# A three-block network on one core: bias tables written from all partitions, key sets joined by pairs of heads, and a scan's products ordered by kind

## The chip, the cores and the metric

The kernel runs on one core of a Trainium2 chip, as one program that a scheduler has laid out beforehand: each engine (TensorE for matmuls, VectorE, ScalarE, GpSimd, and SyncE, which issues DMAs) works off its own list in order and waits on semaphores for the others. The metric is the time of one execution on the device in microseconds. In rows PE is TensorE, PEld its weight loads, DVE VectorE, ACT ScalarE, POOL GpSimd, SP SyncE; a q behind a name is the queue of that engine's sequencer.

## What is computed

A residual block of dilated window attention and a state-space scan, then two blocks with two streams (512 latent tokens, 256 context tokens), the first with an rwkv scan, the second with an mLSTM. All is fp32. Three parts matter here. Attention has 24 heads in three groups of eight; a group has its own window, dilation and table of relative bias. The three groups' outputs of a head are joined by a softmax over their log denominators:

```python
logits = einsum('znqhd,znkhd->znhqk', qb, kw) * HEAD_DIM ** -0.5 + bias
m = max(logits); p = exp(logits - m); den = sum(p)
o, lse = (p @ v) / den, m + log(den)
...
alpha = softmax(stack(lses), axis=2)
attn = sum(alpha[..., None] * stack(outs), axis=2)      # (b, s, 8 * 64)
```

The bias of query i and key j depends on i - j alone (`rel_bias_g[bucket]`, -inf outside the window). The rwkv scan has eight heads of 64 and runs in both directions over the context (256 tokens) and then the latent stream (512):

```python
def step(s, inp):
    r_t, w_t, k_t, v_t, kk_t, b_t = inp
    sa = einsum('bhvk,bhk->bhv', s, kk_t)
    s = s * w_t[:, :, None, :] - sa[..., None] * b_t[:, :, None, :] + v_t[..., None] * k_t[:, :, None, :]
    return s, einsum('bhvk,bhk->bhv', s, r_t)
```

## The kernel before

Big products are split into high and low parts and taken as three matmuls (`mm3`, L301 to L303; `tok`, L384 to L386). `wload` brings a weight block of 128 x 1024 through three rotating buffers: SyncE loads `wraw` (0.52 MB), ScalarE casts `whi` (L292), VectorE subtracts `wlo` (L293). PSUM has eight banks: four in `psA`, two in `psB` and two in `psO`.

The stages, in us of the profiled span: norm to 22; the projection w_v of the values, 12 loads with 24 matmuls of 512 columns each, 22 to 112; the first pair's queries and keys (`qk`) to 160; the units of attention to 354; the join and the product w_ab to 409; the state-space part, its output and feed-forward to 1430; the rwkv scan 1430 to 2220; the rest to 3434. The scan's twelve steps (four of context, eight latent) are interleaved with feed-forward and projection work that a share in `mix0_scan` hands out; the rest of the order is the scheduler's.

**The tables.** `rel_bias` makes one line per head as a matmul of 33 rows (L446: `p` in 8 partitions, 384 or 256 columns), writes it 128 times to DRAM (`scr`, L449) and reads it back with a row length of one less, so that each partition's line is shifted by one (L452, L454: `B0`, `B12`). All of it is issued by GpSimd, beside the projection's loads.

**Attention.** A pair of heads (`hp`) has four units, two for each of two key sets: group 0's local windows, and groups 1 and 2 together. A unit's scores go through VectorE (bias and maximum, L483), ScalarE (exponential with sums), eight transposes on TensorE (L499), copies (L504) and the product with the values (L514). Maxima and sums of all eight heads collect in `st` (128 x 4 x 8 x 4), unnormalised outputs in `Os`. `merge` takes the units in turn with the next pair's `qk`, for the last pair with five of eight `gates`. Then `attn_join` transposes `st` (L585), writes it to DRAM and reads it with heads on partitions (L589, L591), makes weights 8 x 2 x 512 (L599 to L607), writes them (L609), broadcasts them to 64 partitions per head (L614) and joins the two sets (L617 to L619), split into `ah`, `al`. In the caller w_ab is a product of `ah`, `al` with four loads, two feature blocks each, four k-blocks per feature block, one k-block per pair.

**The scan.** A step has `scores` (products of keys and queries, and transposes by matmul with halves of the identity: `vs`, L1516, 16 of 64 columns, and `Ns`, L1527, 32), `inverse` (L1552, L1562, ten rounds of 16 small products) and `serial` (F, U, N and the output O). In rows a record of a 64-wide fp32 product stands twice, so 16 products are 32 records. O takes, for each of eight (direction, pair) blocks, two products with `Sc` (128 rows, L1618) and two with the state `S` (64 rows, L1620), each with its own start and stop:

```python
for d, b in DB:
    for e, h in enumerate(H):
        mm(O[h, d, b], Sc[:, d, e, b, 1], vu[:, d, e, b], start=True, stop=False, ...)
    for e, h in enumerate(H):
        mm(O[h, d, b], AR[d][h, b, 1], S[h, d, b], start=False, stop=True, ...)
```

## Time and profile before

| | us |
|---|---|
| median of three runs (3434.73 to 3446.99) | 3446.86 |
| the profiled execution | 3435.72 |
| its span | 3433.8 |
| TensorE busy | 3209.5 (93%) |
| VectorE, ScalarE, GpSimd busy | 2010.4, 1383.1, 226.9 |

The span leaves 1.9 us of the profiled execution outside. A record of TensorE begins when the product begins; records overlap, so the cost of one in a row of many is the distance from start to start. [...]

### The profile page before, as it was taken

To read this page: it belongs to the slowest core of one execution; us is meant where nothing else is said; L and a number is where in the kernel's file an instruction comes from. 1 tells how busy PE (TensorE), PEld (TensorE's weight loads), DVE (VectorE), ACT (ScalarE), POOL (GpSimd) and SP (SyncE) were. 2 spreads that over 40 slices of the span, in tenths; PEclk is the share of its full clock that TensorE was granted. 3 is DMA by queue.
4 is the path that set the end of the run, shared out by engine and by line. 5 is a ranking of instruction groups with operands and counts; after the bars stand their busy time and mean duration, and the time that the engine had idled before them with its cause. 6 is when DMAs were issued, how large, how long until landed. Compare 5 with 4: busy or idle time off the path is not lost.

```text
span 3433.8 us, 53206 instructions
## 1 busy us (share of the span) xinstructions
PE 3209.5 (93%) x21803; PEld 2567.3 (75%) x21803; DVE 2010.4 (59%) x3226; ACT 1383.1 (40%) x2294; POOL 226.9 (7%) x260
## 2 busy tenths in 40 slices
PE   6999799999889999889899999989999989899998
PEld 5877577777677788766577888767788767778887
DVE  2333567775645543556655656667565754766656
ACT  2233244342344442443344444446532444543323
POOL 0000000000100000022121121000000200000001
PEclk9999999999999999999899999999999989999999
DMA  7411343445444432434555544542322325232323
GB/s 135 128 62 62 109 140 128 135 148 177 148 138 136 128 111 98 139 119 119 151 164 164 169 160 137 177 168 89 108 95 92 133 95 172 89 105 92 98 92 111
DMA packets 216843, 430.96 MB, mean 126 GB/s; under 512 B 75426, under 2 KB 114546, under 8 KB 216344
## 3 DMA queue, kind: packets, MB, share of 16 engines
q1 hardware_dynamic: 193736, 370.09, 34.1%
q10 hardware_dynamic: 20464, 51.58, 4.0%
q0 software_dynamic: 2400, 5.90, 1.7%
q8 instruction: 171, 2.80, 0.3%
q14 instruction: 72, 0.59, 0.1%
HBM read 380.70 MB, written 46.79 MB: 124 GB/s over the span
## 4 chain that ended last, share of the span: by engine, by line
PE 77%; DVE 9%; DMA 7%; ACT 4%; issue 2%; POOL 0%; SPq 0%; ACTq 0%; POOLq 0%; DVEq 0%
PE psa L301 11%; PE psa L303 11%; PE psa L302 11%; PE psa L385 5%; PE psa L384 5%; PE psa L386 5%; PE pso L301 3%; PE pso L303 3%; PE pso L302 3%; DVE wlo L293 2%; DMA wraw<-in_w_v_dram 1%; PE psa L1552 1%; ACT whi L292 1%; PE psa L1562 1%; PE pso L1017 1%
## 5 line engine op out<-in xcount | busy, mean ns | idle before, releaser
L293 DVE TENSOR_TENSOR wlo<-wraw,whi 128x1024 fp32r<-128x1024 f32 x480 | 597.5, 1246 | 524.2 <-ACT whi L292 518.7
L292 ACT CAST whi<-wraw 128x1024 fp32r<-128x1024 f32 x482 | 503.7, 1046 | 773.0 <-PE psa L386 224.6
L301 PE MATMUL psa<-xh,wlo 128*128 128x512 f32 (+1 forms) x1760 | 693.3, 396 | 18.0 <-DVE wlo L293 10.7
L303 PE MATMUL psa<-xh,whi 128*128 128x512 f32 (+1 forms) x1760 | 684.7, 390 | 0.0
L302 PE MATMUL psa<-xl,whi 128*128 128x512 f32 (+1 forms) x1760 | 683.7, 389 | 0.0
L301 PEld LDWEIGHTS psa<-xh,wlo 128*128 128x128 f32 x1760 | 335.6, 192 | 97.6 <-DVE wlo L293 14.9
L303 PEld LDWEIGHTS psa<-xh,whi 128*128 128x128 f32 x1760 | 336.0, 191 | 72.7 <-issue 4.2
L302 PEld LDWEIGHTS psa<-xl,whi 128*128 128x128 f32 x1760 | 336.3, 191 | 71.6 <-issue 3.8
L1138 DVE SCALAR_TENSOR_TENSOR fc<-psa,f_cv,fc 128x441 f32<-128x441 f32 (+2 forms) x352 | 243.4, 692 | 41.4 <-ACT fc L1127 34.5
L301 PE MATMUL pso<-xh,wlo 128*128 128x256 f32 (+1 forms) x720 | 232.0, 322 | 0.6 <-ACT u L1445 0.5
L302 PE MATMUL pso<-xl,whi 128*128 128x256 f32 (+1 forms) x720 | 222.0, 308 | 1.0 <-DVE xl L347 1.0
L303 PE MATMUL pso<-xh,whi 128*128 128x256 f32 (+1 forms) x720 | 221.8, 308 | 0.0
L385 PE MATMUL psa<-wlo,ah 128*128 128x512 f32 x528 | 210.9, 399 | 2.8 <-DVE wlo L293 2.5
L384 PE MATMUL psa<-whi,al 128*128 128x512 f32 x528 | 209.0, 399 | 3.4 <-ACT whi L292 3.4
L386 PE MATMUL psa<-whi,ah 128*128 128x512 f32 x528 | 209.7, 398 | 0.0
L301 PEld LDWEIGHTS pso<-xh,wlo 128*128 128x128 f32 x720 | 137.0, 190 | 12.9 <-issue 1.7
L302 PEld LDWEIGHTS pso<-xl,whi 128*128 128x128 f32 x720 | 136.9, 190 | 9.6 <-DVE xl L347 1.6
L303 PEld LDWEIGHTS pso<-xh,whi 128*128 128x128 f32 x720 | 136.5, 190 | 8.2 <-issue 0.8
L384 PE MATMUL psa<-whi,xl 128*128 128x512 f32 x288 | 117.6, 410 | 19.3 <-ACT whi L292 16.0
L385 PEld LDWEIGHTS psa<-wlo,ah 128*128 128x128 f32 x528 | 99.0, 188 | 30.1 <-DVE wlo L293 6.3
L384 PEld LDWEIGHTS psa<-whi,al 128*128 128x128 f32 x528 | 98.8, 187 | 29.6 <-ACT whi L292 4.7
L385 PE MATMUL psa<-wlo,xh 128*128 128x512 f32 x288 | 117.2, 407 | 1.1 <-DVE wlo L293 1.1
(554 smaller groups left out, 5168.5 us busy)
## 6 DMA issues: line engine op xcount, KB each, us to landing
wraw<-in_f_up_dram SPq DMA_DIRECT2D x132, 512.0 KB, 3.8
wraw<-in_ada_w_dram SPq DMA_DIRECT2D x96, 512.0 KB, 3.6
wraw<-in_f_dn_dram SPq DMA_DIRECT2D x66, 512.0 KB, 3.5
wraw<-in_w_fi_dram SPq DMA_DIRECT2D x44, 512.0 KB, 3.5
wraw<-in_ab_f_dram SPq DMA_DIRECT2D x38, 512.0 KB, 3.8
wraw<-in_w_qk_dram SPq DMA_DIRECT2D x24, 512.0 KB, 3.7
wraw<-in_w_xbc_dram SPq DMA_DIRECT2D x24, 512.0 KB, 4.7
wraw<-in_c_f_dram SPq DMA_DIRECT2D x24, 512.0 KB, 4.3
```

The lines of the kernel that those rows point to most:

```text
L292: nc.scalar.copy(hi, raw)
L293: (eng or nc.vector).tensor_tensor(lo, raw, hi.bitcast(F32), op=ALU.subtract)
L301: mm(ps, wl, xh, start=start, stop=False)
L302: mm(ps, wh, xl, start=False, stop=False)
L303: mm(ps, wh, xh, start=False, stop=stop)
L384: mm(ps, sl, wh[:, c], start=first and k == 0, stop=False)
L385: mm(ps, sh, wl[:, c], start=False, stop=False)
L386: mm(ps, sh, wh[:, c], start=False, stop=last and k == kbn - 1)
L1017: nc.tensor.matmul(ps[o:o + 32], self.cs[:, 4 * h + j, 22 - 2 * i:54 - 2 * i], raw[:, j * 256:(j + 1) * 256], start=h == 0, stop=h == 1, t ...
L1138: V_.scalar_tensor_tensor(o, pv[:, r0 + dr:r1 + dr, c0 + dc:c1 + dc], cw(i), o, op0=ALU.mult, op1=ALU.add)
L1552: mm(ps[h, d, b], Al[h, d, b], Tm[h, d, b], start=True, stop=True, tile_position=(64 * e, 64 * e))
L1562: mm(ps[h, d, b], lt[h, d, b], rt[h, d, b], start=True, stop=True, tile_position=(64 * e, 64 * e))
```

## The change

Three parts. In `rel_bias` each head's line is replicated over 16 partitions before the matmul (`rep`, one copy of 33 x 24 x 16 more), so that the table stands in all 128 partitions, each of which writes 8 of a head's 128 copies. `attn_join` is called per pair: its statistics are 32 x 128, its tables 8 x 128 (head and chunk of 128 tokens on partitions), its DMAs are issued by ScalarE (one and four for `dstat`) and GpSimd; a pair's join is merged with the next pair's units, the last with the last four gates (four where five stood beside the last units). w_ab makes two rounds of two loads and four banks: three k-blocks for all four, then the last pair's k-block. In the scan O takes all `Sc` products and then all `S` products with one start and stop per bank, and `vs` and `Ns` are made with whole transposes of 128 x 128: 4 and 8 in place of 16 and 32 half ones; the copies of `vs` become four smaller ones, two of them on VectorE.

```diff
@@ rel_bias
-        tab, es = flat()[:NBUCKET + 1, :896], flat()[:8]
+        tab, es = flat()[:NBUCKET + 1, :896], flat()
+        rep = pool.tile([NBUCKET + 1, 24, 16], F32, name="pT", bufs=3)
+        nc.vector.tensor_copy(rep, lhs.unsqueeze(2).to_broadcast([NBUCKET + 1, 24, 16]))
...
-            ps = self.btile()[:8, :L]
-            nc.tensor.matmul(ps, lhs[:, g * 8:(g + 1) * 8], tab[:, off:off + L], start=True, stop=True)
+            ps = self.btile()[:, :L]
+            nc.tensor.matmul(ps, rep[:, g * 8:(g + 1) * 8].rearrange("k h r -> k (h r)"), tab[:, off:off + L], start=True, stop=True)
...
-            scr = self.dram.tile([8, P * L + 512], F32, name="scr%d" % g)
-            dst = scr[:, :P * L].rearrange("h (p l) -> h p l", l=L)
-            nc.gpsimd.dma_start(dst, e.unsqueeze(1).to_broadcast([8, P, L]))
+            scr = self.dram.tile([8, P * L], F32, name="scr%d" % g)
+            dst = scr.rearrange("h (r q l) -> (h r) q l", q=8, l=L)
+            nc.gpsimd.dma_start(dst, e.unsqueeze(1).to_broadcast([P, 8, L]))
@@ attention
             for hp in range(4):
-                merge(units(hp, *qk_[hp]), qk(hp + 1, *qk_[hp + 1]) if hp < 3 else islice(other, 5))
-          with self.tc.tile_pool(name="ac", bufs=2) as pool:
-              merge(self.attn_join(pool, st, Os, ah, al), other)
+                Os = op.tile([P, 2, SEQ], F32, name="Os", bufs=2)
+                merge(units(hp, *qk_[hp], Os), qk(hp + 1, *qk_[hp + 1]) if hp < 3 else islice(other, 4), join)
+                join = self.attn_join(op, hp, st[:, hp], Os, ah, al)
+          merge(join, other)
@@ attn_join, the part after the change
+        ps = self.btile()[:32, :P]
+        nc.tensor.transpose(ps, st.rearrange("p a e c -> p (a e c)"), self.ident)
+        sT = pool.tile([32, P], F32, name="sT")
+        S_.copy(sT, ps)
+        dst = self.dram.tile([4, 2, 4, P], F32, name="dstat%d" % hp)
+        S_.dma_start(dst[0:2].rearrange("a e c p -> (a e c) p"), sT[0:16])
+        for x in range(4):
+            S_.dma_start(dst[2 + x // 2, x % 2].rearrange("c (r i) -> r c i", r=4),
+                         sT[16 + 4 * x:20 + 4 * x].rearrange("r (c i) -> r c i", c=4))
+        yield
+        R = pool.tile([8, 4, P], F32, name="R")
+        G_.dma_start(R, dst.rearrange("a e c p -> (e c) a p"))
...
+        S_.activation(W[:, :, 0], W[:, :, 0], AF.Exp)
         yield
...
+        G_.dma_start(dw.rearrange("s e c p -> (e c) s p"), W[:, :, 0])
         yield
...
+        Wb = pool.tile([P, 2, SEQ], F32, name="Wb")
+        for e in range(2):
+            G_.dma_start(Wb[64 * e:64 * e + 64], dw[:, e].rearrange("s c p -> s (c p)").unsqueeze(0).to_broadcast([64, 2, SEQ]))
+        yield
+        y, z = Os[:, 0], Os[:, 1]
+        V_.tensor_tensor(y, y, Wb[:, 0], op=ALU.mult)
...
+        self.split(ah[:, hp], al[:, hp], y)
@@ block1_, w_ab
-                    for s in range(4):
-                        w = self.wload(D["w_ab"], s, 1)
-                        for j in range(2):
-                            fb = 2 * s + j
-                            ps = self.ptile()
-                            self.feat(ps, w, 0, (ah, al), kbn=4, off=j * 512)
+                    for s in range(2):
+                        w = self.wload(D["w_ab"], 2 * s)
+                        pss = [self.ptile() for _ in range(4)]
+                        for j, ps in enumerate(pss):
+                            self.feat(ps, w, j // 2, (ah, al), kbn=3, off=j % 2 * 512, last=False)
+                        for j, ps in enumerate(pss):
+                            fb = 4 * s + j
+                            self.feat(ps, w, j // 2, (ah, al), kbn=1, kbx=3, off=j % 2 * 512 + 384, first=False)
@@ rwkv_scan, scores
-            ps = v8(self.btile())
-            for d, b in DB:
-                for e in range(2):
-                    mm(ps[H[1 - e], d, b], v[d][:, b], ident[e], start=True, stop=True,
-                       tile_position=(0, 64 * (1 - e)))
+            ps = self.btile().rearrange("p (d q c) -> p d q c", d=2, q=2)
+            for d in range(2):
+                for q in range(2):
+                    nc.tensor.transpose(ps[:, d, q], v[d][:, 2 * q:2 * q + 2].rearrange("p b t -> p (b t)"), self.ident)
             for e in range(2):
-                S_.copy(vs[H[1 - e], :, e], ps[H[1 - e]])
+                o = vs[H[1 - e], :, e].rearrange("p d (q o) v -> p d q o v", o=2)
+                for h in range(2):
+                    (S_.copy, V_.tensor_copy)[h ^ e](o[:, :, :, h], ps[H[h], :, :, H[e]])
...
-            for e in range(2):
-                ps = v8(self.btile())
-                for d, b in DB:
-                    for k in range(2):
-                        o = e if k == 0 else 1 - e
-                        mm(ps[H[o], d, b], KB[d][:, b, k ^ e], ident[e], start=True, stop=True,
-                           tile_position=(0, 64 * o))
-                S_.copy(Ns[:, :, e], ps)
+            for d in range(2):
+                ps = self.btile().rearrange("p (b c) -> p b c", b=4)
+                for b in range(4):
+                    nc.tensor.transpose(ps[:, b], KB[d][:, b].rearrange("p k t -> p (k t)"), self.ident)
+                S_.copy(Ns[:, d].rearrange("p e b k -> p b e k"), ps.rearrange("p b (e k) -> p b e k", e=2))
@@ rwkv_scan, serial
-                    mm(O[h, d, b], Sc[:, d, e, b, 1], vu[:, d, e, b], start=True, stop=False, tile_position=(0, 64 * e))
+                    mm(O[h, d, b], Sc[:, d, e, b, 1], vu[:, d, e, b], start=d + b == 0, stop=False, tile_position=(0, 64 * e))
+            for d, b in DB:
                 for e, h in enumerate(H):
-                    mm(O[h, d, b], AR[d][h, b, 1], S[h, d, b], start=False, stop=True, tile_position=(64 * e, 64 * e))
+                    mm(O[h, d, b], AR[d][h, b, 1], S[h, d, b], start=False, stop=d + b == 4, tile_position=(64 * e, 64 * e))
```

What this does to the order is seen at three places. On TensorE, the end of a latent step's output and the transposes of the step after next, before (`vu`, `Sc`, `S`, `AR` are operands of O; `v` is what `vs` is made from; `Tm`, `Al` belong to the inverse):

```order
L1618 MATMUL psb<-vu,Sc 64x64 x2
L1620 MATMUL psb<-S,AR_11401 64x64 x2
L1618 MATMUL psb<-vu,Sc 64x64 x2
L1620 MATMUL psb<-S,AR_11401 64x64 x2
L1516 MATMUL psb<-masks,v_13002 64x64 x8
L1516 MATMUL psb<-masks,v_13008 64x64 x8
L1552 MATMUL psa<-Tm,Al 64x64 x16
```

and the same place after the change (L1370 and L1375 are work from the other stream that was between O's products before, too):

```order
L1573 MATMUL psa<-W,X 64x64 x16
L1629 MATMUL psb<-vu,Sc 64x64 x11
L1370 MATMUL pso<-wda,up 128x512
L1375 MATMUL pso<-wda,up 128x512
L1629 MATMUL psb<-vu,Sc 64x64 x5
L1632 MATMUL psb<-S,AR_11395 64x64 x8
L1632 MATMUL psb<-S,AR_11401 64x64 x8
L1529 MATMUL psb<-masks,v_12934 128x128 x2
L1529 MATMUL psb<-masks,v_12940 128x128 x2
L1563 MATMUL psa<-Tm,Al 64x64 x16
```

The products of one kind now stand together, and four transposes stand for sixteen. On GpSimd, from the tables to the end of attention, before:

```order
L449 DMA scr_227<-p 8x128x384
L449 DMA scr_233<-p 8x128x256
L452 DMA B_216<-scr_227 128x8x256
L454 DMA B_217<-scr_233 128x8x128
L449 DMA scr_239<-p 8x128x256
L464 MEMSET p 128x2x128
L454 DMA B_217<-scr_239 128x8x128
L464 MEMSET p 128x2x128 x3
```

and after, to the end of the first pair's join:

```order
L452 DMA scr_228<-p 1024x1x384
L452 DMA scr_234<-p 1024x1x256
L455 DMA B_215<-scr_228 128x8x256
L457 DMA B_216<-scr_234 128x8x128
L452 DMA scr_240<-p 1024x1x256
L467 MEMSET p 128x2x128
L457 DMA B_216<-scr_240 128x8x128
L467 MEMSET p 128x2x128
L602 DMA R<-dstat_1254 8x4x128
L618 DMA dw_1355<-R 8x2x128
L622 DMA Wb<-dw_1355 64x2x512 x2
L467 MEMSET p 128x2x128
```

The tables' DMAs keep their places, and between the memsets of the units (`p`) each join's DMAs have come in. On VectorE, the end of the only join before (`W`, `tm` are the weights' tables, `g` a gate, `ay`, `az` the products):

```order
L606 RECIPROCAL tm<-tm 8x512
L829 TENSOR_SCALAR g_206<-g_206 128x512
L607 TENSOR_TENSOR W<-W,tm 8x1024
L293 TENSOR_TENSOR wlo<-wraw,whi 128x1024
L617 TENSOR_TENSOR ay<-Os,Wb 128x512
L618 TENSOR_TENSOR az<-Os,Wb 128x512
L619 TENSOR_TENSOR ay<-ay,az 128x512
L318 TENSOR_TENSOR al<-ay,ah 128x512
```

and the end of the last pair's join after:

```order
L293 TENSOR_TENSOR wlo<-wraw,whi 128x1024
L615 TENSOR_TENSOR R<-R,M 8x128
L616 TENSOR_TENSOR R<-R,M 8x32x4
L839 TENSOR_SCALAR g_205<-g_205 128x512
L293 TENSOR_TENSOR wlo<-wraw,whi 128x1024
L839 TENSOR_SCALAR g_206<-g_206 128x512
L625 TENSOR_TENSOR Os<-Os,Wb 128x512
L627 TENSOR_TENSOR Os<-Os,Wb 128x512
L293 TENSOR_TENSOR wlo<-wraw,whi 128x1024
L629 TENSOR_TENSOR Os<-Os 128x512
L318 TENSOR_TENSOR al<-Os,ah 128x512
```

The tables are a quarter as wide, and one pair's products stand there instead of four.

## Rows read from the trace of the kernel before

**Rows 1.** Windows, five stretches: us, engines' busy time, granted clock, DMA share, GB/s
```profile
core 0: us, PE busy (x) PEld busy (x) DVE busy (x) ACT busy (x) POOL busy (x), PEclk, DMA share, GB/s
30.00:50.00 20.00, 20.00 (x89) 17.36 (x88) 6.26 (x7) 2.45 (x3) 0.00 (x0) 1.00 0.96 54
160.00:354.00 194.00, 190.60 (x1071) 140.74 (x1071) 71.38 (x197) 78.20 (x188) 0.94 (x3) 1.00 0.19 61
402.00:408.00 6.00, 6.00 (x28) 4.98 (x27) 2.61 (x3) 1.05 (x1) 0.00 (x0) 1.00 0.83 246
1430.00:1700.00 270.00, 227.77 (x2629) 168.34 (x2628) 175.99 (x254) 113.25 (x194) 57.20 (x62) 0.89 0.43 121
1700.00:2200.00 500.00, 484.89 (x6967) 411.47 (x6966) 303.67 (x456) 226.89 (x385) 84.89 (x89) 1.00 0.50 161
```

**Rows 2.** Timeline of TensorE, projection and first qk: start, duration, line, idle before
```profile
45.44 0.40 PE L384 MATMUL psa<-whi,xl 128*128 128x512 f32 x1
...
56.49 0.40 PE L386 MATMUL psa<-whi,xh 128*128 128x512 f32 x1
72.87 0.82 PE L384 MATMUL psa<-whi,xl 128*128 128x512 f32 x1 [15.98 <-ACT whi L292]
...
114.10 0.68 PE L301 MATMUL psa<-xh,wlo 128*128 128x512 f32 x1 [3.09 <-DVE V L532]
...
117.85 0.39 PE L301 MATMUL psa<-xh,wlo 128*128 128x512 f32 x1
```

**Rows 3.** Timeline of ScalarE and GpSimd in the projection, idle time before in brackets
```profile
71.77 1.04 ACT L292 CAST whi<-wraw 128x1024 fp32r<-128x1024 f32 x1 [30.48 <-DMA wraw<-in_w_v_dram]
...
82.90 0.93 POOL L452 DMA_DIRECT2D B<-scr  x1 [53.07 <-DMA scr<-p]
```

**Rows 4.** Timeline of TensorE, VectorE and SyncE at the join and w_ab
```profile
352.31 0.33 PE L585 MATMUL psb<-masks,st 128*128 128x128 f32 x1
...
354.11 0.33 SPq L589 DMA_DIRECT2D dstat<-sT  x1
355.65 0.33 SPq L591 DMA_DIRECT2D R<-dstat  x1
...
360.48 1.07 DVE L599 TENSOR_TENSOR tm<-R 8x512 f32<-8x512 f32 x1
...
373.00 0.30 SPq L609 DMA_DIRECT2D dw<-W  x1
...
374.81 12.18 SPq L614 DMA_DIRECT2D Wb<-dw  x8
...
380.56 0.69 DVE L617 TENSOR_TENSOR ay<-Os,Wb 128x512 f32<-128x512 f32 x1 [6.45 <-DMA Wb<-dw]
383.62 0.79 PE L301 MATMUL psa<-ah,wlo 128*128 128x512 f32 x1 [15.01 <-ACT ah L317]
...
404.63 0.39 PE L301 MATMUL psa<-ah,wlo 128*128 128x512 f32 x1
...
408.48 0.39 PE L303 MATMUL psa<-ah,whi 128*128 128x512 f32 x1
```

**Rows 5.** Timeline of TensorE in the latent scan's step 3
```profile
2005.77 1.15 PE L1516 MATMUL psb<-masks,v 128*64 128x64 f32 x32
...
2031.71 1.15 PE L1605 MATMUL psb<-vu,Ns 128*64 128x64 f32 x32
2032.79 1.15 PE L1562 MATMUL psa<-W,X 64*64 64x64 f32 x32
...
2036.87 0.34 PE L1618 MATMUL psb<-vu,Sc 128*64 128x64 f32 x4
...
2040.98 1.10 PE L1552 MATMUL psa<-Tm,Al 64*64 64x64 f32 x32
```

**Rows 6.** Timeline of TensorE in attention, eight transposes of a unit
```profile
342.54 1.03 PE L499 MATMUL psb<-masks,p 128*128 128x128 f32 x8
```

**Rows 7.** VectorE's copy at line 1593 in the scan: ns, first to last
```profile
L1593 DVE COPY f<-psb x12: 402/418/425, 1460.7 to 2195.6; 128x256 f32<-128x256 f32 x12
```

More of the change, by code (lines that the diff above doesn't have):

```diff
@@ L522, in attention @@
         with self.tc.tile_pool(name="ao", bufs=1) as op:
-          st = op.tile([P, 4, 8, 4], F32, name="st")
-          Os = op.tile([P, 4, 2, SEQ], F32, name="Os")
+          st = op.tile([P, 4, 4, 2, 4], F32, name="st")
+          join = iter(())
           with self.tc.tile_pool(name="at", bufs=2) as pool:
@@ L550, in qk, with units @@
                         yield
-            def units(hp, qT, kT):
+            def units(hp, qT, kT, Os):
                 last = None
@@ L557, in units @@
                     for half in range(2):
-                        u = self.attn_unit(pool, hp, sid, half, qT, kT, V, (B0, B12)[sid], st, O)
+                        u = self.attn_unit(pool, hp, sid, half, qT, kT, V, (B0, B12)[sid], st[:, hp], O)
                         next(u)
@@ L578, in attn_end, with attn_join @@
         if half:
-            self.nc.scalar.copy(Os[:, hp, sid], O)
-    def attn_join(self, pool, st, Os, ah, al):
+            self.nc.scalar.copy(Os[:, sid], O)
+    def attn_join(self, pool, hp, st, Os, ah, al):
         nc = self.nc
-        ps = self.btile()[:, :P]
-        nc.tensor.transpose(ps, st.rearrange("p a b c -> p (a b c)"), self.ident)
-        sT = pool.tile([P, P], F32, name="sT", bufs=1)
-        nc.vector.tensor_copy(sT, ps)
-        dst = self.dram.tile([4, 8, 4, P], F32, name="dstat")
-        nc.sync.dma_start(dst.rearrange("a b c p -> (a b c) p"), sT)
-        R = pool.tile([8, 4, SEQ], F32, name="R", bufs=1)
-        nc.sync.dma_start(R, dst.rearrange("a b c p -> b a (c p)"))
+        V_, S_, G_ = nc.vector, nc.scalar, nc.gpsimd
+        ps = self.btile()[:32, :P]
[10 more added lines that the diff above has]
+        G_.dma_start(R, dst.rearrange("a e c p -> (e c) a p"))
@@ L602, in attn_join @@
-        S_.activation(W, W, AF.Exp)
-        V_.tensor_tensor(L, W[:, 0], R[:, 1], op=ALU.mult)
-        V_.tensor_tensor(n(M), n(W[:, 1]), v(3), op=ALU.mult)
-        V_.tensor_tensor(L, L, M, op=ALU.add)
-        V_.reciprocal(L, L)
-        V_.tensor_tensor(W, W, L.unsqueeze(1).to_broadcast([8, 2, SEQ]), op=ALU.mult)
-        dw = self.dram.tile([8, 2, SEQ], F32, name="dw")
-        nc.sync.dma_start(dw, W)
-        yield
-        for hp in range(4):
-            Wb = pool.tile([P, 2, SEQ], F32, name="Wb")
-            for e in range(2):
-                nc.sync.dma_start(Wb[64 * e:64 * e + 64], dw[2 * hp + e].unsqueeze(0).to_broadcast([64, 2, SEQ]))
-            y = pool.tile([P, SEQ], F32, name="ay")
-            z = pool.tile([P, SEQ], F32, name="az")
-            V_.tensor_tensor(y, Os[:, hp, 0], Wb[:, 0], op=ALU.mult)
-            V_.tensor_tensor(n(z), Os[:, hp, 1].rearrange("d (r i) -> d i r", r=4), n(Wb[:, 1]), op=ALU.mult)
-            V_.tensor_tensor(y, y, z, op=ALU.add)
-            self.dump("attnT%d" % hp, y)
-            self.split(ah[:, hp], al[:, hp], y)
-            yield
+        M = pool.tile([8, P], F32, name="M")
@@ new lines, in attn_join @@
+        V_.tensor_tensor(n(M), n(R[:, 0]), v(2), op=ALU.max)
+        V_.tensor_tensor(R[:, 0], R[:, 0], M, op=ALU.subtract)
+        V_.tensor_tensor(v(2), v(2), n(M), op=ALU.subtract)
+        W = R.rearrange("h (s k) p -> h s k p", k=2)
+        S_.activation(W[:, :, 0], W[:, :, 0], AF.Exp)
+        yield
+        V_.tensor_tensor(W[:, :, 1], W[:, :, 0], W[:, :, 1], op=ALU.mult)
+        V_.tensor_tensor(n(M), n(R[:, 1]), v(3), op=ALU.add)
+        V_.reciprocal(M, M)
+        V_.tensor_tensor(R[:, 0], R[:, 0], M, op=ALU.mult)
@@ new lines, in attn_join @@
+        V_.tensor_tensor(v(2), v(2), n(M), op=ALU.mult)
+        dw = self.dram.tile([2, 2, 4, P], F32, name="dw%d" % hp)
+        G_.dma_start(dw.rearrange("s e c p -> (e c) s p"), W[:, :, 0])
+        yield
+        Wb = pool.tile([P, 2, SEQ], F32, name="Wb")
[4 more added lines that the diff above has]
+        V_.tensor_tensor(y, y, Wb[:, 0], op=ALU.mult)
@@ L624, in dt_stage @@
+        zv = z.rearrange("d (r c i) -> d r c i", r=4, c=4)
+        V_.tensor_tensor(zv, zv, Wb[:, 1].rearrange("d (c r i) -> d r c i", r=4, c=4), op=ALU.mult)
+        yv = y.rearrange("d (i r) -> d i r", r=4)
+        V_.tensor_tensor(yv, yv, z.rearrange("d (r i) -> d i r", r=4), op=ALU.add)
+        self.dump("attnT%d" % hp, y)
+        self.split(ah[:, hp], al[:, hp], y)
+        yield
     def dt_stage(self, xT, pool, tmp):
@@ L1466, in rwkv_scan @@
         DB = [(d, b) for d in range(2) for b in range(4)]
-        ident = [self.ident[:, h] for h in H]
         q8 = lambda a: a.rearrange("p d b t -> p (d b) t")
```

14 lines of the change are left out of this document (3 added, 11 removed).

## The prediction

> **What bounds the kernel now.** I read the table of windows first, then TensorE's timeline in the three places that the diff touches, then what ended each wait. TensorE (PE in the rows) is the bound nearly everywhere: in attention it is busy 190.6 of 194 us, in the latent half of the rwkv scan 484.9 of 500, both at a granted clock of 1.00 [rows 1]. So work taken off TensorE there is worth about its own length, and work moved to another engine is free as long as that engine waits for TensorE. Three stretches are otherwise. In the w_v projection TensorE stops for 15.98 us at 72.87 although its work is there [rows 2]; at the join of attention's key sets it stops for 15.01 us at 383.62 [rows 4]; in the context half of the scan it is busy only 227.8 of 270 us at a clock of 0.89 [rows 1].
>
> The profiled execution took 3435.7 us, 11 less than the median of the runs shown (3446.9; two of the three lie there, one at 3434.7). I sum against 3435.7 and come back to the 11 at the end.
>
> **The tables of attention's bias.** Each of three tables is written to DRAM with every head's line repeated, then read back shifted. Before, the repeats leave from 8 partitions. The second read waits on GpSimd's queue until 82.90, 53.07 us behind the writes [rows 3]; the first two writes hold 8 x 128 x (384 + 256) x 4 bytes = 2.62 MB, so they went at some 49 GB/s. In 30 to 50 us the DMA engines are busy 0.96 of the time and move 54 GB/s in all [rows 1]. They are full, and yet slow: at 402 to 408 us they move 246 GB/s at 0.83 [rows 1]. The weight loads share them, and a cast of one waits 30.48 us for its load [rows 3]. That is why TensorE stands.
>
> What is it worth? Twelve loads of 24 matmuls make the projection. Between 45.44 and 56.49 there are 47 intervals of 0.235 us [rows 2], and at 56.72 (one interval after 56.49) six loads are used up. The other six are 144 x 0.235 = 33.8 us, so an unhindered projection ends at 90.6. In fact the next stage's first matmul is at 114.10, 23.5 us later, and its first nine run at the lower clock, 3.75 us to 117.85 [rows 2] where nine take 9 x 0.2265 = 2.0 (0.2265 is the pitch of 17 matmuls from 404.63 to 408.48 [rows 4]): 1.7 more. The most to be had is 25.2 us. After the change the repeats leave from 128 partitions: 3.67 MB for all three tables, 15 us at the 246 GB/s of rows 1, while a load of 0.52 MB is wanted every 24 x 0.2265 = 5.4 us (96 GB/s). Both fit, so I take -25. At half that rate the writes last 30 us and two of the loads in that time come some 5 us late each: -15, the weak bound. A loss I exclude: the matmul has as many columns as before, and one copy of 33 x 384 is added.
>
> [...]
>
> **The join of the key sets.** Before, one join for all heads runs after the last unit. Its chain: the transpose of the statistics at 352.31, a write at 354.11, a read at 355.65, the first table step at 360.48, the weights' write at 373.00, the broadcasts at 374.81, the first product at 380.56, the first matmul on it at 383.62 [rows 4]. The gates fill TensorE until 368.61 (15.01 before 383.62), and w_ab ends at about 408.7: 40.1 us for 96 matmuls, which are 21.7 at 0.2265. So 18.4 is the most.
>
> After, three pairs' joins run beside the next pair's units, and only the fourth's chain is exposed. I rebuild it from rows 4: 1.8 to the write, five issues of 0.33 where one was and a landing like 355.65 - 354.11 = 1.5, together 3.2; the read, issue to first table step, 4.8; tables of 128 columns where 512 took 373.00 - 360.48 = 12.5, about 4; write 1.8; broadcasts 5.8; products and split 380.56 to 383.62, 3.1. That is 24.5, and about 27 if GpSimd's queue is slower at issuing than SP's (0.93 per issue in rows 3 against 0.33). The cover behind the transpose is, in the order of the changed kernel, 82 gate matmuls and the 36 w_ab matmuls on heads already joined (of the first two units of w_ab, kbn=3): 118 x 0.2265 = 26.7. So it is close. I take -15; the bounds are -10 and -18. If the cover fails, TensorE waits for what is left of the chain and no more.
>
> The price is inside attention: each of three pairs adds a copy and five DMA issues on ScalarE, some eight steps on VectorE, and four issues on GpSimd. ScalarE is busy 78.2 and VectorE 71.4 of 194 us there [rows 1]. Both work in order, so a product that waits for its broadcast holds back the weights' low parts (wlo) and the bias steps queued behind it, and TensorE waits for those. At 1 us a pair I take +3; 0 if the broadcast has landed before, 10 if each pair's product waits half of the 6.45 us of rows 4.
>
> **The scan.** Each of twelve steps is costed at full clock from step 3. The output's 32 products alternate in groups of four between two tile shapes (128 x 64 and 64 x 64) and last from 2036.87 to 2040.98, 4.11 us; a block of 32 of one shape takes 2031.71 to 2032.79, 1.08 [rows 5]. By kind, 16 and 16, there is one change of shape instead of fifteen: 1.08 if the change is free, and as the dear end twice that, 2.16, a whole block's start for each kind. I take the dear one. Saved: 4.11 - 2.16 = 1.95 (3.0 at the other end). The transposes are three blocks of 32 records now (one for vs, two for Ns; [rows 5] shows the first, 1.15), 3 x 1.08 = 3.24; after, twelve whole 128 x 128 transposes, and eight of that shape take 1.03 [rows 6], so 12 x 0.129 = 1.55. Saved: 1.7. Together 3.6 a step. Eight latent steps lie where TensorE is the bound: 29, of which I take nine tenths, 26. Four context steps lie where it idles a sixth of the time: 14.6, half of it, 7.3. So -33.5; the bounds are -20 (no gain in the context half, two thirds in the other) and -45 (all of it).
>
> VectorE takes two of the copies of vs: 24 x 0.418, by the nearest copy [rows 7], 10 us over the scan, where it is busy 303.7 of 500 us and 176 of 270 [rows 1]. In the latent half this hides. In the context half it may not, which is in the half that I took.
>
> **Sum.** -25 - 15 + 3 - 33.5 = -70.5: 3435.7 - 70.5 = 3365. The 11 us by which the runs shown exceed the profiled one are weighed by a quarter, so 3368.
>
> **The rivals.** (1) The writes are slow for another reason than their 8 partitions: their pieces stay 1.0 to 1.5 KB, and the same queue carries them. Then the tables' 25 us stay: 3393. For it speaks that nothing in the trace shows such a write from 128 partitions; against it, that the reads back of 1 KB pieces are not in the wait of 53.07. 9 in 100.
> (2) The join's waits come back: the last chain outlasts its cover by 15 us, and each pair's product holds VectorE. 3368 + 15 + 7 = 3390. For it: the cover is even with my chain, and the queues work in order. 11 in 100.
> (3) The scan doesn't follow TensorE: its serial chain goes through ScalarE and VectorE copies, and what TensorE saves becomes idle time. 3368 + 25 = 3393. Against it: 484.9 of 500. 6 in 100.
> Two of these: about 3415, 2 in 100; all three: 3437, 4 in 100 (they share my reading that TensorE's time is the kernel's).
> (4) Slower. In the scan matmuls are replaced by half as many whole transposes, and TensorE's clock falls. The scan's clock is 0.96 now (0.89 over 270 us, 1.00 over 500 [rows 1]), TensorE busy for 712.7 us. With the other two parts as forecast and no gain in the scan the time is 3399; a mean clock of 0.90 gives 712.7 x (0.96/0.90 - 1) = 48 us back and ends level with before, which is where it decides, and 0.87 gives 74: 3473. Against it: attention, with eight transposes in each of sixteen units, is granted 1.00 [rows 1]. 4 in 100.
> [...]
>
> **How the numbers follow.** The forecast has 64 in 100. Its own ends are 3435.7 - 25 - 18 - 45 = 3348 and 3435.7 - 15 - 10 - 20 + 10 = 3401. I take 3343 to 3404, which also holds rivals 1 to 3 and leaves out the rest, 10 in 100, and tails. About 0.5% is what a measurement of this kernel can tell from no change, 3429.6 to 3464.1: faster 0.64 + 0.09 + 0.11 + 0.06 + 0.02 = 0.92, within 0.04, slower 0.04.
>
> **What will show it.** Tables right: no wait over 3 us in the projection, the qk stage's first matmul at about 90, the DMA engines far above 54 GB/s while the tables are written. Join right: between the gates' last matmul and w_ab's first less than 1 us, w_ab's end 40 us or more earlier than before (25 + 15); wrong if a wait of over 5 us stands ahead of w_ab's last k-block. Scan right: the output's block at most 2.2 us, eight transposes in about 1, and the stage from its first to its last step some 33 us shorter; a block that is shorter in a stage that is not says rival 3. A mean granted clock under 0.93 there says rival 4. Outside the three places nothing should move by more than 3 us; if it does, the prediction is wrong in what it left out.

## The result and the profile after

The changed kernel takes 3386.3 us in the median of four runs (3376.7 to 3392.8) against 3445.3 before: a ratio of 0.9833 with the 95% interval [0.9801, 0.9865], 59 us less. On the same chip as later kernels it took 3389.7 (ratio 0.9845 [0.9823, 0.9866]). Its profiled execution took 3376.7, span 3375.0; it is the fastest of the four. The median is inside the range of 3343 to 3404, and 18 us short of the forecast 3368.

The places of the change in the trace after. First the tables and the projection: windows (columns as in [rows 1]) while the tables are written, GpSimd's second read, and the qk stage's first matmul, which answers to 114.10 in [rows 2]:

```profile
28.00:34.00 6.00, 6.00 (x27) 4.74 (x27) 1.65 (x2) 1.05 (x1) 1.11 (x2) 1.00 0.98 358
34.00:41.00 7.00, 7.00 (x32) 5.80 (x31) 1.23 (x1) 1.94 (x2) 1.44 (x2) 1.00 0.99 321
```

```profile
34.70 0.92 POOL L455 DMA_DIRECT2D B<-scr  x1 [5.59 <-DMA scr<-p]
...
90.44 0.40 PE L301 MATMUL psa<-xh,wlo 128*128 128x512 f32 x1
```

The DMA engines are as full as before (a share of 0.98 after 0.96) but move 358 GB/s in all where they moved 54, and the first read waits 5.59 us in place of 53.07. TensorE no longer waits in the projection, where 15.98 us stood.

The join, TensorE's timeline: the first and the last matmul of w_ab, the one that needs the last pair, and the first that needs the next weights (`MT`):

```profile
341.90 0.39 PE L301 MATMUL psa<-ah,wlo 128*128 128x512 f32 x1
...
350.97 0.50 PE L302 MATMUL psa<-al,whi 128*128 128x512 f32 x1 [0.23 <-DVE al L318]
...
364.25 0.39 PE L303 MATMUL psa<-ah,whi 128*128 128x512 f32 x1
...
375.64 0.61 PE L301 MATMUL psa<-xh,MT 128*32 128x512 f32 x1 [5.56 <-DVE MT L318]
```

The wait of 15.01 us in [rows 4] is 0.23 now. Another, of 5.56, stands behind w_ab. ScalarE's queue issues the load of `MT` late; the rows of this queue after, and the same load before:

```profile
371.07 0.78 ACT L698 ACTIVATE cacc<-psa,convb,conv 128x512 f32<-128x512 f32 x1 [5.34 <-DMA accd<-g]
371.10 0.37 ACTq L641 DMA_DIRECT2D MT<-in_w_dt_dram  x1
```

```profile
412.40 0.42 ACTq L631 DMA_DIRECT2D MT<-in_w_dt_dram  x1
```

The scan, the same kind of step as in [rows 5]: the output's block, and four transposes of `vs` with what follows them.

```profile
2044.37 1.15 PE L1629 MATMUL psb<-vu,Sc 128*64 128x64 f32 x32
2045.45 1.15 PE L1632 MATMUL psb<-S,AR 64*64 64x64 f32 x32
2046.43 0.28 PE L1563 MATMUL psa<-Tm,Al 64*64 64x64 f32 x3
...
2014.34 0.60 PE L1529 MATMUL psb<-masks,v 128*128 128x128 f32 x4
2014.87 1.15 PE L1573 MATMUL psa<-W,X 64*64 64x64 f32 x32
```

The output takes 2046.43 - 2044.37 = 2.06 us (4.11 before), four transposes 0.53. So TensorE's work shrank about as worked out. What became of it is seen by cutting the scan at its first, fourth and eighth output block. Windows of before, then of after:

```profile
1428.00:1508.20 80.20, 68.14 (x921) 54.17 (x920) 47.73 (x88) 37.55 (x83) 16.38 (x17) 0.91 0.33 110
1508.20:1749.70 241.50, 209.54 (x2364) 152.39 (x2363) 159.10 (x208) 103.51 (x174) 49.49 (x52) 0.91 0.48 134
1749.70:1982.00 232.30, 222.69 (x3261) 188.10 (x3259) 138.10 (x218) 99.93 (x174) 41.87 (x45) 0.99 0.53 170
1982.00:2246.00 264.00, 256.76 (x3469) 215.62 (x3468) 163.76 (x242) 115.99 (x178) 34.34 (x37) 0.99 0.50 162
```

```profile
1392.90:1476.60 83.70, 68.92 (x754) 53.85 (x753) 49.97 (x92) 37.50 (x83) 17.38 (x17) 0.84 0.32 105
1476.60:1711.10 234.50, 197.87 (x2110) 144.58 (x2109) 162.79 (x214) 102.44 (x174) 48.01 (x52) 0.89 0.49 138
1711.10:1941.90 230.80, 212.14 (x2929) 179.89 (x2925) 143.65 (x226) 97.93 (x174) 41.66 (x45) 0.97 0.52 171
1941.90:2191.60 249.70, 241.38 (x3215) 204.99 (x3214) 163.51 (x249) 114.17 (x179) 37.54 (x38) 0.99 0.53 172
```

The second number is the stretch's length, the third TensorE's busy time; the last three are the granted clock (PEclk, a share of the full one), the DMA share and GB/s. Over the four, TensorE is busy 757.1 us before and 720.3 after, 36.8 less; it is idle 60.9 before and 78.4 after, 17.5 more. The stage is 19.3 shorter in these two traces. The last stretch passes its saving on (15.4 busy, 14.3 in length) and the second a good half of it (11.7 and 7.0). In the third, 10.6 us of work less shorten it by 1.5; the first is 3.5 longer.

The granted clock fell as well. The whole scan in one window each: before, after, and two kernels of the next section, `u_transp` (the changed kernel with the half transposes of before) and `u_output` (the changed kernel with the output's products in the order of before):

```profile
1428.00:2246.00 818.00, 757.13 (x10009) 610.29 (x10008) 508.69 (x754) 356.99 (x609) 142.09 (x151) 0.96 0.49 151
1392.90:2191.60 798.70, 720.31 (x8999) 583.31 (x8998) 519.92 (x778) 352.04 (x609) 144.59 (x151) 0.94 0.49 155
1392.90:2194.70 801.80, 733.26 (x10009) 598.53 (x10008) 509.01 (x754) 355.98 (x609) 144.11 (x151) 0.96 0.49 154
1388.90:2206.10 817.20, 747.28 (x9001) 599.66 (x9000) 520.01 (x778) 353.69 (x609) 141.16 (x151) 0.94 0.49 151
```

The two kernels with half transposes are granted 0.96 over the scan, the two with whole ones 0.94.

### The profile page after: what moved, and what is told of

It reads as the page before. It is cut to its first block, busy times and chain, and to the rows that moved or that the text cites. A ratio compares the mean times of both kernels' runs of the same rounds, so it can differ in the third digit from the quotient of the medians.

```text
span 3375.0 us, 51306 instructions
## 1 busy us (share of the span) xinstructions
PE 3163.2 (94%) x20798; PEld 2539.0 (75%) x20798; DVE 2023.6 (60%) x3274; ACT 1378.6 (41%) x2301; POOL 238.0 (7%) x276
## 4 chain that ended last, share of the span: by engine, by line
PE 76%; DVE 10%; DMA 6%; ACT 4%; issue 3%; POOL 1%; SPq 0%; ACTq 0%; POOLq 0%; DVEq 0%
PE psa L301 11%; PE psa L303 11%; PE psa L302 11%; PE psa L384 6%; PE psa L385 6%; PE psa L386 6%; PE pso L301 3%; PE pso L302 3%; PE pso L303 3%; DVE wlo L293 3%; PE psa L1563 1%; ACT whi L292 1%; PE psa L1573 1%; PE pso L1030 1%; PE pso L384 1%
## 5 line engine op out<-in xcount | busy, mean ns | idle before, releaser
L301 PEld LDWEIGHTS pso<-xh,wlo 128*128 128x128 f32 x720 | 136.4, 189 | 11.9 <-issue 1.7
```

The costliest lines, as they stand in the source:

```text
L301: mm(ps, wl, xh, start=start, stop=False)
```

## The experiments

Three undo one part of the change each, by its lines in the diff; the times are medians, against 3386 to 3390 for the changed kernel. Traces of one kernel differ: the changed kernel's two have spans of 3375.0 and 3389.2 us, at mean granted clocks of 0.972 and 0.967. So parts are read from their own stages.

**Tables as before** (`rel_bias` of the old kernel).

> The changed kernel with the bias tables as before (written from 8 partitions). Theory, parts add up: the qk stage's first matmul goes back from 90 to 114 us, the wait of about 16 us in the projection comes back, and the time is some 24 us above the changed kernel's (about 3410 against 3386). Rival, the join's gain leans on the tables (its last chain is short only while the DMA queue is free): the join's stage loses too, 35 us or more.

3421.1 us (ratio 0.9938 [0.9919, 0.9957]). The first qk matmul comes at 115.9, the projection's wait is 17.0, the first unit comes 27 us later than in the changed kernel. The join's stage loses 2 to 3 us more than that (29.6 at the first transpose of the state-space part). That is more than the theory's 24 and less than the rival's 35; by medians it is 31 to 35 us, with some 10 on either side. Whether the two parts simply add up is not settled.

**One join as before.**

> The changed kernel with one join for all heads, as before. Theory: the stage from the first units to the end of w_ab is 15 us longer, 3401 or so; 15 us of waiting stand ahead of w_ab and the 5.6 us ahead of its last k-block go. Rival, the pairs' joins cost attention a few us that are hidden in this 15: the units' stage would then be 3 us or more shorter than in the changed kernel, once its one gate more is allowed for.

3397.8 us. The state-space part starts 10.1 us later than in the changed kernel, not 15: the wait of 15.02 us ahead of w_ab is back, but the one for `MT` behind it falls to 2.03, and from w_ab's end to the state-space part it is 24.4 us, as before the change. From the first unit to the last row of products with the values it takes 201.1 us, the changed kernel 198.9; a gate more is 24 x 0.2265 = 5.4, so the pairs' joins cost attention 3.2 by this pair of traces, as the rival has it. The kernel before (204.0, with the same gate) gives 0.3. The other kernels that join by pairs and have four gates there take 196.8 to 200.9, so neither figure is clear of the spread, and the price stays open.

**The scan as before.**

> The changed kernel with the scan as before. Theory, half of what TensorE saves in the scan became waiting: the scan's stage is 19 us longer, 3405, TensorE busy some 37 us more and idle 17 less in it. Rival, the scan gave its 33.5 and something else (the stages from 409 to 1430) lost 14: this kernel is then at 3420 and has its stages before the scan as the kernel before.

3398.1 us. Scan start to scan end 815.1 us (818.0 before). Four traces with the changed scan (the changed kernel twice, the two above) give 798.7, 804.9, 802.4 and 801.9, mean 802.0: the change of the scan is worth 13 to 16 in the traces, and 8 to 12 by the medians. The stages before the scan are as in the changed kernel within 1.4, so the rival falls.

**Which half of the scan's change.** First the transposes undone, then the output's order undone.

> The changed kernel with the half transposes as before (output by kind kept). Theory, the new waiting comes with the transposes (their copies on VectorE, and the loads of keys that they set free): undoing them costs 5 us or less against the changed kernel, though TensorE is busy 20 us more. Rival, the waiting comes of any shortening of TensorE's work, whichever: it costs about 9, in proportion to its 20 of 45 us.

```diff
-            ps = self.btile().rearrange("p (d q c) -> p d q c", d=2, q=2)
-            for d in range(2):
-                for q in range(2):
-                    nc.tensor.transpose(ps[:, d, q], v[d][:, 2 * q:2 * q + 2].rearrange("p b t -> p (b t)"), self.ident)
+            ps = v8(self.btile())
+            for d, b in DB:
+                for e in range(2):
+                    mm(ps[H[1 - e], d, b], v[d][:, b], ident[e], start=True, stop=True,
+                       tile_position=(0, 64 * (1 - e)))
...
```

3390.7 us, scan 801.8: the whole transposes are worth nothing that can be told from the spread, though TensorE is busy 13 us longer without them (733.3). The scan's start, to the first output block, is 77.6 us where the changed kernel takes 83.7: they cost 6 us there and give it back over the later steps. Without them the clock is that of before (0.96 over the scan).

> The changed kernel with the output's products alternating by block as before (whole transposes kept). Theory: each output block is 4.1 us again and the scan's stage 14 us longer (what undoing the scan costs, 17, less the 3 of the transposes): about 3400. Rival, the two edits of the scan share one gain (either alone brings most of it): under 8 us.

```diff
-                    mm(O[h, d, b], Sc[:, d, e, b, 1], vu[:, d, e, b], start=d + b == 0, stop=False, tile_position=(0, 64 * e))
-            for d, b in DB:
+                    mm(O[h, d, b], Sc[:, d, e, b, 1], vu[:, d, e, b], start=True, stop=False, tile_position=(0, 64 * e))
                 for e, h in enumerate(H):
-                    mm(O[h, d, b], AR[d][h, b, 1], S[h, d, b], start=False, stop=d + b == 4, tile_position=(64 * e, 64 * e))
+                    mm(O[h, d, b], AR[d][h, b, 1], S[h, d, b], start=False, stop=True, tile_position=(64 * e, 64 * e))
```

3397.8 us, scan 817.2: by the traces the output's order by kind carries all of the scan's gain, 15 of the 12 x 2.05 = 24.6 us that it takes off TensorE; by medians on one chip it is 8. The clock stays at 0.94, so its fall goes with the whole transposes and not with the order of the output. It is not their waits alone: in the second stretch this kernel idles 32.4 us at a clock of 0.89, `u_transp` 33.9 at 0.92 (`u_transp` first).

```profile
1470.50:1705.70 235.20, 201.34 (x2364) 148.12 (x2363) 159.90 (x208) 103.30 (x174) 48.60 (x52) 0.92 0.49 138
1473.30:1710.90 237.60, 205.23 (x2112) 149.00 (x2111) 162.71 (x214) 102.60 (x174) 48.55 (x52) 0.89 0.49 136
```

The changed kernel once more, as the measure of these four:

> The changed kernel itself, unaltered, on the same chip as the next three, as their measure: 3386, within 8 either way, and the same stage lengths in its trace as before within 1 us.

3389.7, scan 804.9, clock 0.93 over it; the stretches of the scan agree within 2.5 us but for the third (235.5 against 230.8), against the 1 us that I expected.

**What makes the scan start late.** Two suspects, one kernel each.

> The changed kernel with all four copies of vs on ScalarE. Theory, the scan's start is late because VectorE works in order and its two copies stand ahead of the next projection's normalisation: the first output block comes at 1471 instead of 1476.6, and the whole is 4 to 6 us faster. Rival, the loads of keys (one buffer) hold the scores, and these hold VectorE: the first output block stays at 1476, and the whole within 3 us.

```diff
-                    (S_.copy, V_.tensor_copy)[h ^ e](o[:, :, :, h], ps[H[h], :, :, H[e]])
+                    S_.copy(o[:, :, :, h], ps[H[h], :, :, H[e]])
```

3390.7 us, the first output block 86.4 us after the scan's start: no gain, the copies on VectorE are not the cause.

> The changed kernel with two buffers for the keys KB (and the output's copy in the buffer of f, for the room). Theory, a load wait blocks VectorE at the start: the waits of TensorE for KB (5.1 us over the scan) go, the first output block comes at 1471, 5 us faster; later steps gain what they wait for KB. Rival, the copies on VectorE do it: no change over 2 us at the first output block.

```diff
-                KB = first.tile([P, 4, 2, 64], F32, name="KB%d" % d, bufs=1)
+                KB = first.tile([P, 4, 2, 64], F32, name="KB%d" % d, bufs=2)
...
-            y = pool.tile([P, 2, 4, 64], F32, name="yo", bufs=1)
+            y = new("f", 1)
```

3384.4 us (ratio 0.9828 [0.9811, 0.9845]); the first output block comes after 78.4 us. TensorE's waits in that start, changed kernel and this one (us in total, times, longest):

```profile
PE pso L338 <- DVE xl L347: 5.5, 4, 2.5
PE psa L1513 <- DMA KB<-zk: 5.1, 2, 3.3
```

```profile
PE pso L338 <- DVE xl L347: 6.3, 4, 3.2
PE pso L338 <- DVE xn L332: 1.3, 1, 1.3
```

The wait for the keys is gone and 5.3 to 5.9 us with it. The output's copy, which this edit moves for the room, is not the reason: `ar3` below moves it too, and its start takes 84.2. On VectorE in the changed kernel the wait for the keys is passed on: a step of the scan that needs the scores stood 2.77 us, and the next projection's normalisation (`xl`) behind it. How much that adds is not shown, since TensorE's wait for `xl` is no shorter with two buffers (6.3 against 5.5).

```profile
1413.01 0.69 DVE L1516 TENSOR_TENSOR Sc<-psa,masks 128x512 f32<-128x512 f32 x1 [2.77 <-PE psa L1513]
1413.61 0.34 DVE L347 SCALAR_TENSOR_TENSOR xl<-pso,modt,xh 128x128 fp32r<-128x128 f32 x1
```

The start with two buffers against the one with half transposes:

```profile
1392.20:1470.60 78.40, 66.47 (x754) 51.95 (x753) 50.13 (x92) 37.35 (x83) 17.62 (x17) 0.89 0.35 112
1392.90:1470.50 77.60, 66.39 (x921) 52.71 (x920) 47.80 (x88) 37.50 (x83) 16.34 (x17) 0.93 0.35 113
```

TensorE idles about as long in both (11.9 and 11.2 us), and the clock is still lower with the whole transposes.

**What eats the third stretch.**

> The changed kernel with three buffers for AR instead of two (and the output's copy in the buffer of f, for the room). Theory, between the fourth and the eighth output block TensorE's saved time turns into waiting because the load of AR starts when the output's last product lets its buffer go and has 5 us less of TensorE's work to hide behind: with a third buffer the waits for AR (5.4 to 6.9 us there) go, and the stretch from the fourth to the eighth output block falls from 231 to 235 us to about 227. Rival, the step's own chain (VectorE's Tm, GpSimd's copies) is the limit there: the waits for AR go and others of the same length take their place, and the stretch stays within 2 us.

```diff
-                AR = first.tile([P, 4, 2, 64], F32, name="AR%d" % d)
+                AR = first.tile([P, 4, 2, 64], F32, name="AR%d" % d, bufs=3)
...
-            y = pool.tile([P, 2, 4, 64], F32, name="yo", bufs=1)
+            y = new("f", 1)
```

3379.6 us (ratio 0.9818 [0.9796, 0.984]). The third stretch takes 224.4 us, and no wait for AR stands in it. This is clear of the spread: the eight traces with the new order of the output and two buffers for AR take 230.8 to 237.0 there, and `best`, below, which has three buffers too, 222.0. With the old order it is 232.3 to 234.7 (before, `u_scan`, `u_output`), so that without the third buffer the new order gains nothing here. The copy that the edit moves is not the reason: with it and two buffers for AR (`kb2`) the stretch takes 237.0. TensorE's longest waits there before, in the changed kernel, and with three buffers, in us in total, times, longest:

```profile
PE psa L1552 <- DVE Tm L1565: 5.1, 2, 4.6
PE psa L1501 <- DMA AR<-za: 1.9, 1, 1.9
```

```profile
PE psa L1513 <- DMA AR<-za: 5.4, 2, 4.2
PE psa L1563 <- DVE Tm L1576: 5.2, 4, 3.7
```

```profile
PE psa L1563 <- DVE Tm L1576: 5.5, 4, 3.8
PE psb L1529 <- DVE S L1619: 2.6, 1, 2.6
```

The wait for `Tm` is about the same in all three; the wait for AR grows with the change and goes with the buffer. (A wait for `S`, 0.4 us before, is 2.8 in the changed kernel and stays with three buffers.) In the kernel with the old order of the output the wait for AR is 1.9 us, as before: alternating products let the first direction's AR go half a block, 2 us, before the end; by kind both go in the last half microsecond. SyncE's issue of the load shows it, before (2.0 us ahead of the block's end at 1862.82) and after (0.3 ahead of 1819.13):

```profile
1860.87 2.42 SPq L1480 DMA_DIRECT2D AR<-za  x2
```

```profile
1818.82 0.80 SPq L1492 DMA_DIRECT2D AR<-za  x2
```

**Three mends at once**, a miss (two buffers for KB, the state products of the output ahead of the others, three gates beside the last units in place of four):

> The changed kernel with two buffers for KB, the output's state products ahead of its score products (AR is let go one half block earlier) and three gates beside the last units instead of four. Theory, each mends a wait: 6 us at the scan's start, 1 us at two loads of AR, and the 5.6 us ahead of the last k-block of w_ab; together 10 us, about 3378. Rival, a gate taken from the last units leaves TensorE idle there by as much as it covers later: from the last units to w_ab's end no change, 6 us in all.

3390.4 us. The scan's start gained its 4; the other two brought nothing. With the state products first the load of AR was issued 1.2 us earlier (1817.65), but its matmul still waited 6.3 us, to 1826.76: the landing took longer (9.1 us from its issue to that matmul, 6.4 in the changed kernel), and why is not settled. The gate that was taken from the last units made them 6 us shorter, but w_ab starts at 340.5, where the other kernels with the new tables and joins by pairs start it (339.7 to 344.2): the gate runs behind the units instead. The 5.6 us stayed. They do not stand ahead of w_ab's last k-block, as I had read the row, but behind w_ab, at the load of `MT`.

**Half the partitions.**

> The changed kernel with the tables written from 64 partitions (8 replicas of a head, 16 copies each) instead of 128. [...] Rival, the rate goes with the number of partitions up to what the engines can do: 64 is eight times the 8 that moved 54, and the rate stays at 340 to 360. [...]

```diff
-            dst = scr.rearrange("h (r q l) -> (h r) q l", q=8, l=L)
-            nc.gpsimd.dma_start(dst, e.unsqueeze(1).to_broadcast([P, 8, L]))
+            dst = scr.rearrange("h (r q l) -> (h r) q l", q=16, l=L)
+            nc.gpsimd.dma_start(dst, e.unsqueeze(1).to_broadcast([64, 16, L]))
...
```

3384.5 us in one run; the qk stage starts at 90.7. The windows of the table writes, to be read against the first two rows of this section's beginning:

```profile
28.00:34.00 6.00, 6.00 (x27) 4.44 (x26) 1.64 (x2) 1.05 (x1) 1.29 (x2) 1.00 0.96 225
34.00:41.00 7.00, 7.00 (x32) 5.81 (x31) 1.22 (x1) 1.70 (x2) 0.93 (x1) 1.00 0.99 235
```

54, 225 and 358 GB/s while 8, 64 and 128 partitions are read, the weight loads included, at DMA shares of 0.96 to 0.98 each: not in proportion to the partitions (64 is eight times 8, and four times as much is moved; 128 is twice 64, and 1.6 times as much is moved, 1.4 in the second window). The 225 and 235 are 0.63 and 0.73 of what the changed kernel moves in the same windows, so the rival's 340 to 360 did not come. Why the rate goes this way with the partitions, no run shows.

**A version that beats both.** From ar3, the weights behind w_ab loaded through the weights' ring:

> The changed kernel with three buffers for AR and the output's copy in f's buffer (as in ar3), and the weights of dt, 128 x 256, loaded through the weights' ring (SyncE's queue) instead of into memory that the gates hold until their last write has landed. Theory, what the join gains is in part given back at the next load: TensorE's wait of 5.6 us behind w_ab goes or falls under 2, the stretch from w_ab's end to the first transpose of the state-space part (364 to 394 in the changed kernel) is 4 us shorter, and the whole is 4 us faster than ar3, about 3376, some 2.0% under the kernel before. Rival, the convolution's statistics that follow wait for the same memory (hc and the next tiles), so another wait of the same length takes its place: 3380.

```diff
-        raw = tmp.tile([P, 256], F32, name="MT", bufs=3)
-        nc.scalar.dma_start(raw, D["w_dt"])
-        hi = tmp.tile([P, 8, 32], F32R, name="MT", bufs=3)
-        lo = tmp.tile([P, 8, 32], F32R, name="MT", bufs=3)
+        raw = self.wp.tile([P, 1024], F32, name="wraw")[:, :256]
+        nc.sync.dma_start(raw, D["w_dt"])
+        hi, lo = (self.wp.tile([P, 1024], F32R, name="w" + n)[:, :256] for n in ("hi", "lo"))
...
```

3364.3 us in the median of five, ratio to before 0.9777 [0.976, 0.9794]: 81 us less. From w_ab's end to the first transpose of the state-space part, the changed kernel and this one:

```profile
364.30:394.00 29.70, 24.14 (x99) 16.61 (x97) 13.76 (x18) 9.06 (x14) 0.00 (x0) 0.89 0.29 96
```

```profile
362.30:384.50 22.20, 22.20 (x99) 16.11 (x97) 13.68 (x18) 9.64 (x13) 0.00 (x0) 1.00 0.45 146
```

The wait is gone, and so is the stretch at the lower clock behind it (0.89 over the first row, 1.00 over the second): 7.5 us, more than I expected (4). The median is 15 under that of ar3, and the trace 13; 4 of the 13 stand ahead of w_ab and are no part of the edit. What is beyond the 7.5 I do not explain.

## Why the prediction was right, and where it was off

**Tables, -25: right.** The first qk matmul came at 90.44 (forecast 90.6), 23.7 earlier; with the stretch at the lower clock gone (0.54 granted from 114.10 to 117.85 before, 1.00 from 90.40 to 94.00 after) it is 25.4 at the first unit. That writes from 128 partitions would go faster was my estimate, which no row of before showed; the runs bear it out: from 8 partitions the DMA engines moved 54 GB/s, from 64 and 128 four and six times that, with pieces of the same size on the same queue. Whether it is the partitions themselves or how such a transfer is spread over the DMA engines no run parts; that the mean share of all 16 was 0.96 speaks against a few engines. The rate (246 taken from a busy stretch elsewhere) was too low against 358, which changed nothing, since the projection had room. Rival 1 is out.

**Join, -15 + 3: the sum right, in part by luck, the terms off.** w_ab ends 44.2 us earlier (408.48 to 364.25); less the tables' 25.4 that is 18.8, the whole bound of 18.4. The last chain was covered but for 0.23; it took 29.0 us (the transpose at 321.93, the product at 350.97) where 24.5 to 27 were summed, and its cover was longer than the 26.7 too, so the even balance held by luck. The price in attention, +3, came out between 0.3 and 3.2, not clear of the spread. Rival 2 is out: its two prices together were 22. What the prediction missed comes behind: where a wait goes, what is late next. The next stage's weights were loaded late, when the last gates had been written (ScalarE's queue issues them at 371.10, 6.8 us after w_ab; in the kernel before 3.9 after). From w_ab's end to the state-space part it is 29.7 us where it was 24.6: 5.1 given back, 13.7 left, close to the forecast 12 because a term that was left out and a gain that was sized too low cancel. That the gates' memory is what held the load is inferred from the row on ScalarE's queue ([5.34 <-DMA accd<-g]); that the late load is the cause is shown by the last run.

**Scan, -33.5: the wrong size; 13 to 19 came.** Its terms on TensorE were right (2.06 for the output against 2.16, 0.53 for four transposes against 0.52), and TensorE was busy 36.8 us less. The step that failed is "Eight latent steps lie where TensorE is the bound: 29, of which I take nine tenths": of these 26 us 15.8 came, and 8.7 in the changed kernel's second trace. I read that from one window of 500 us, busy 484.9. Cut at the steps, its halves look alike, 9.6 us idle in 232 and 7.2 in 264; but in the first a load of AR was already late by 1.9 us, and nothing but work on TensorE hid the rest of it. The saving was kept in the last steps and in a good half of the second stretch. In the third it was eaten by the loads of AR, which the new order of the output lets go later; at the start by the loads of KB. Both are named by a run that takes them away (ar3, kb2). So rival 3 came true in half of the scan, but mostly not by its reason: the chain through `Tm` is no longer than before, loads are (only the wait for `S`, 2.4 us more in the third stretch, is of the rival's kind). The context steps gave 3.5 to 4.4 where 7.3 were forecast. The transposes, which I had priced at 20 of the 44 us, gave nothing in time: against `u_transp` TensorE is busy 13 us less and idle 10 us more, at a lower clock.

**Rival 4 came true in part.** The kernel is not slower, and the clock over the scan is not under the 0.93 that I had named as its sign; but it fell, from 0.96 to 0.94 and 0.93 in the changed kernel's two traces, and it did so with the whole transposes: in the kernel before and in `u_transp`, with half ones, which are matmuls with halves of the identity, it is 0.96 with either order of the output. By my own price, 712.7 x (0.96/0.94 - 1), a fall to 0.94 costs 15 us, about what the scan fell short; my sum had put this at nothing. That price takes TensorE as the bound throughout, and the waits above are in the same shortfall, so the two overlap, and how they share it is not shown. The fall lies in the first two stretches, where TensorE also waits (0.91 to 0.84 and 0.91 to 0.89, with 14.8 and 36.6 us idle after). Rows with about as much idle time part the two: 0.92 with half transposes and 0.89 with whole ones in the second stretch, 0.93 and 0.89 at the start (`kb2`). In the last stretch, with next to no waiting (7.2 us idle before, 8.3 after), the clock is 0.99 with either. That the transposes themselves lower it is not shown: no run changes them alone, without the copies and loads behind them.

**Outside the change.** From the state-space part's first transpose to the scan the changed kernel took 998.9 us, before 994.9; other traces of changed kernels lie between 995 and 1003. The 4 us in my sum's disfavour are of the size of that spread, and with one trace of before their cause stays open. Trace against trace the account is -25.4 - 13.7 + 4 - 19.3 - 4.4 (behind the scan) = -58.8. The two terms outside the change, +4 and -4.4, are over the 3 us that I had set as the sign of something left out. With the changed kernel's second trace the account is -37.5 (tables and join) + 4.4 - 13.1 + 1.6 = -44.6: the term behind the scan changes its sign, so it is spread. Of the 18 us by which the forecast was short, the scan has 14 by the first trace, tables and join gave 2 back, and some 7 come from the end of the sum: I took a quarter of the 11 us between trace and median, while the trace after was the fastest of its four and the median stands 10 us above it.

## What to carry to other kernels

A busy share does not say what a saving is worth: of two stretches with TensorE busy 96 and 97%, one passed on a seventh of it at best, the other eight to nine tenths. Ask at each step which load lands last and how much work hides it. When products are put into another order, look at what each of them lets go: with AR read last, its load was issued 0.3 us ahead of the block's end where it had been 2.0. When a wait is removed, look for the next load behind it and ask when its buffer comes free; here a third buffer for AR took 6 us or more off its stretch and one load through another queue 7.5 off its own. Compare the clock of kernels with and without a new kind of instruction over the whole stage, not in its fullest stretch alone: over the scan it was 0.94 here against 0.96, in its last stretch 0.99 in both.

## What was not expected of the hardware

DMA engines that read 8 partitions show a busy share of 0.96 while they move 54 GB/s, and the cast of a weight block waited 30.48 us for its load from DRAM. With the same write from 64 and from 128 partitions they moved 225 and 358 GB/s at shares of 0.96 and 0.98: the share did not tell the rate. On TensorE, 32 products that change tile shape every two products took 4.11 us, sorted by shape 2.06, so that a change cost (4.11 - 2.06) / 14 = 0.15 us, more than the two products themselves (0.13). The start and stop flags changed with the order, but they are not what costs: in the sorted block products begin 0.058 us apart, and at its one change of shape two of these distances are 0.158 and 0.107, again 0.15 more. And kernels whose scan uses whole transposes were granted a mean clock of 0.94 or 0.93 in it, the kernel before and `u_transp` with half ones 0.96.
